# A transformer block's prelude: modulation weights by column halves, three pieces summed on TensorE, thirteen on VectorE

## The chip, the cores and the metric

The kernel runs on one core of a Trainium2 chip. The time is the device time of one execution in microseconds (us); lower is better. Times are medians over runs of the same kernel on the same inputs. The profile shows one execution, recorded by the hardware profiler. TensorE (PE) multiplies matrices, VectorE (DVE) and ScalarE (ACT) work element by element, GpSimd (POOL) does a few operations beside them, and SyncE (SP) issues the DMA transfers.

## The reference

The reference is one block of a hybrid model: sequence 1024, width 1024, batch 1, all in fp32. Cut to what matters here:

```python
mod = jax.nn.silu(c) @ w_mod[l] + b_mod[l]            # c is [1, 1024], w_mod [1024, 6144]
shift1, scale1, gate1, shift2, scale2, gate2 = jnp.split(mod, N_MOD, axis=-1)
u = modulate(rms_norm(h, ln1_g[l]), shift1, scale1)   # xn * (1 + scale) + shift
proj = u @ w_in                                        # then split: attention, RWKV, gates
...
h = h + gate1[:, None, :] * mix
u2 = modulate(rms_norm(h, ln2_g[l]), shift2, scale2)
h = h + gate2[:, None, :] * conv_ffn(u2, ...)
return rms_norm(h, final_g)
```

Nothing can be multiplied by `w_in` before `u` is there, and `u` needs `shift1` and `scale1`: 2048 columns of `w_mod`, 8 MB. This stretch, from the start to the first products with `w_in`, is the prelude.

## The kernel before, in words

**Form of the data.** `u` is held channel by row: `xn`, `u_hi` and `u_lo` are tiles of 128 partitions x 8 groups of channels (`kt`) x 1024 tokens. A number is split into a rounded part (`hi`, of type fp32r) and the rest (`lo`), and a product of two such numbers is three fp32r matmuls: hi by hi, lo by hi, hi by lo. A *block* `n` of the prelude is one `kt` and one half of the tokens (512); there are 16.

**The prelude's order.** It stands in one `with` block in which the order of SP, VectorE and ScalarE is the order of the program text (PE's is so in the whole kernel). Behind this block a scheduler orders VectorE, ScalarE, POOL and SP. The steps:

- `load_x` (L424) brings eight tiles of x, 128 tokens x 1024 channels, 512 KB each. `mod_load` (L428) brings sixteen pieces of `w_mod`, 128 rows x 1024 columns each: eight of the shift, then eight of the scale. `low_load` (L432) brings two weights of `w_in`, numbers 24 and 25. Buffers: three for pieces (`mw`), four shared by x tiles 0 to 3 and later pieces (`xa`), four for x tiles 4 to 7 and then one split weight (`xb`). A load into `xa` waits until the first four x tiles have been transposed.
- `square` (L438) and `norm_x` (L444) give each token its root mean square and scale x by it; `turn` (L450) transposes it on PE, four 128 x 128 transposes into a PSUM tile of two buffers, and ScalarE copies that to `xn`.
- `mod_add` (L455, L457) on VectorE multiplies a piece, row by row, by silu(c) and adds it to an accumulator, one for the shift and one for the scale. `mod_sum` sums an accumulator over its 128 partitions by one-column matmuls against ones; `mod_col` (L467, L469) adds the bias and forms `A1`, the factor of the modulation, and `m1`.
- `warm` issues matmuls whose result isn't used, into the PSUM tile `idle`.
- For each block: `u_full` scales and shifts `xn` on VectorE (L483) and casts it to `u_hi` on ScalarE (L484); `u_lower` takes the rest to `u_lo` on VectorE (L488); `low_part` multiplies the block by the three parts of weight 24 and of weight 25, into the PSUM tiles `low`. These are 96 matmuls, "the low matmuls" below. `low_split` (L499, L500) splits these two weights.
- Behind the blocks: `w2` is cast (`w2h`, ScalarE) and its rest taken on POOL (`w2l`), and `low_out` evicts the products.

**What follows.** The large matmuls with the other weights of `w_in` (`ps_rkv` in the profile) begin right behind the low matmuls on PE. Each weight comes through `load_w`: a load into `raw` (two buffers, also used by weights 24 and 25 and by `w2`), a cast on ScalarE (L268), the rest on VectorE (L270). Each use is 24 matmuls for 512 tokens.

Of the kernel before, what the change touches and what calls it, by code (L numbers as in the profile page):

```python
# [15 lines left out]
D = 1024  # L16
S = 1024
KT = 8
# [117 lines left out]
def hybrid_block(ctx: ExitStack, tc: tile.TileContext, a, out):  # L136
# [205 lines left out]
    with ExitStack() as es:  # L342
# [67 lines left out]
        with tc.tile_pool(name="st", bufs=1) as st, tc.tile_pool(name="stp", bufs=2, space=PS) as stp, \  # L410
# [3 lines left out]
            acc = [st.tile([128, D], F32, name=f"acc{seg}") for seg in range(2)]  # L414
            junk = acc[1]
            xn = st.tile([128, KT, S], F32, name="xn")
            xs, pieces = [], {}

            def ring(tag, name, dt=F32):
                return st.tile([128, D], dt, tag=tag, name=name, bufs=3 if tag == "mw" else 4)  # L420

            def load_x(t):
                xs.append(ring("xa" if t < 4 else "xb", f"xt{t}"))
                nc.sync.dma_start(xs[t], a["x"][t * 128 : t * 128 + 128, :])  # L424

            def mod_load(seg, ci):
                w = pieces[seg, ci] = ring("mw" if len(pieces) % 7 < 3 else "xa", f"wm{seg}{ci}")
                nc.sync.dma_start(w, a["w_mod"][ci * 128 : ci * 128 + 128, seg * D : seg * D + D])  # L428

            def low_load(i):  # L430
                raw = rp.tile([128, D], F32, tag="raw", name=f"raw_in{i}")
                nc.sync.dma_start(raw, a["w_in"][i])  # L432
                if i == 24:
                    return raw, *(wp.tile([128, D], F32R, tag=f"w{h}", name=f"{h}_in{i}", bufs=2) for h in ("hi", "lo"))
                return raw, *(ring("xb", f"{h}_in{i}", F32R) for h in ("hi", "lo"))

            def square(t):
                nc.scalar.activation(junk, xs[t], AF.Square, accum_out=ssq[:, t : t + 1])  # L438

            def norm_x(half):  # L440
                hs = slice(half * 4, half * 4 + 4)
                rms_rstd(rstd[:, hs], ssq[:, hs])
# [3 lines left out]
            def turn(kt, half):  # L446
# [3 lines left out]
                nc.scalar.copy(xn[:, kt, half * NH : half * NH + NH], ps)  # L450

            def mod_add(seg, ci, cols=slice(0, D)):
                w, s_ = pieces[seg, ci][:, cols], sc[:, ci : ci + 1]
                if ci == 0:
                    ts(acc[seg][:, cols], w, s_, None, op0=ALU.mult)  # L455
                else:
                    stt(acc[seg][:, cols], w, s_, acc[seg][:, cols], op0=ALU.mult, op1=ALU.add)  # L457

            def mod_sum(seg, k0, n):
                ps = pb.tile([128, NH], F32, tag="big", name=f"mod{seg}{k0}")  # L460
                for k in range(k0, k0 + n):
                    mm(ps[:, k : k + 1], acc[seg][:, k * 128 : k * 128 + 128], ones[:, 0:1], start=True, stop=True)
                return ps

            def mod_col(seg, k0, n, ps):
                k1 = slice(seg * 8 + k0, seg * 8 + k0 + n)
                tt(m1[:, k1], ps[:, k0 : k0 + n], V("b_mod", seg * 8 + k0, n), op=ALU.add)  # L467
                if seg:
                    stt(A1[:, k0 : k0 + n], m1[:, k1], 1.0, V("ln1_g", k0, n), op0=ALU.add, op1=ALU.mult)  # L469

            def warm(n, w=None):
                for _ in range(n):
                    if w is None:
                        mm(idle[:, 0:NC1], cst[:, 0:128], cst, start=True, stop=True)
                    else:
                        mm(idle, ones, w[:, 0:NH], start=True, stop=True)
# [4 lines left out]
            def u_full(n):  # L481
                kt, _, cs = block(n)
                ts(xn[:, kt, cs], xn[:, kt, cs], A1[:, kt : kt + 1], m1[:, kt : kt + 1], op0=ALU.mult, op1=ALU.add)  # L483
                nc.scalar.copy(u_hi[:, kt, cs], xn[:, kt, cs])  # L484

            def u_lower(n):
                kt, _, cs = block(n)
                tt(u_lo[:, kt, cs], xn[:, kt, cs], f32(u_hi[:, kt, cs]), op=ALU.subtract)  # L488

            def low_part(j, n):  # L490
                kt, half, cs = block(n)
                _, wh, wl = low[j]
                for i, (w, x) in enumerate(((wh, u_hi), (wl, u_hi), (wh, u_lo))):
# [3 lines left out]
            def low_split(j):  # L497
                raw, hi, lo = low[j]
                nc.scalar.copy(hi, raw)  # L499
                tt(lo, raw, f32(hi), op=ALU.subtract)  # L500
# [14 lines left out]
            order = [(seg, ci) for seg in range(2) for ci in range(KT)]  # L515
            for t in range(4):
                load_x(t)
            for m in range(3):
                mod_load(*order[m])
            for t in range(4, 8):  # L520
                load_x(t)
            warm(16)
            low = []

            def add_ahead(m):
                if m + 7 < 16:
                    if m + 7 == 14:
                        low.append(low_load(24))
                    mod_load(*order[m + 7])
                mod_add(*order[m])  # L530

            for t in range(4):
                square(t)
            norm_x(0)
            for m in range(3):
                mod_add(*order[m])
            for kt in range(KT):
                turn(kt, 0)
            for m in range(3, 10):
                mod_load(*order[m])  # L540
            for t in range(4, 8):
                square(t)
            for m in (3, 4):
                add_ahead(m)
            norm_x(1)
            for kt in range(KT):
                turn(kt, 1)
            nc.scalar.preload_act_table_set("sigmoid_and_others")
            for m in range(5, 15):
                add_ahead(m)  # L550
                if m == 7:
                    shift_ps = mod_sum(0, 0, KT)
                if m == 9:
                    mod_col(0, 0, KT, shift_ps)
                if m > 10:
                    warm(1, pieces[order[m]])
            low.append(low_load(25))
            low_ps = [[stp.tile([128, NH], F32, tag="low", name=f"low{j}{hf}", bufs=4) for hf in range(2)] for j in range(2)]
            low_split(0)
            halves_ = (slice(0, NH), slice(NH, D))  # L560
            for x in range(2):
                mod_add(1, KT - 1, halves_[x])
            scale_ps = [mod_sum(1, x * 4, 4) for x in range(2)]
            mod_col(1, 0, 4, scale_ps[0])
            u_full(0)
            mod_col(1, 4, 4, scale_ps[1])
# [6 lines left out]
            for n in range(16):  # L573
                if n < 15:
                    u_full(n + 1)
                u_lower(n)
                low_part(0, n)
                if n == 2:
                    low_split(1)
                if n == 3:  # L580
                    for m in range(3):
                        low_part(1, m)
                if n > 2:
                    low_part(1, n)
# [1421 lines left out]
```

## Time and profile before

| | us |
|---|---|
| median of 3 runs | 1670.34 |
| lowest and highest | 1670.2, 1674.31 |
| profiled execution, as timed | 1675.3 |
| its span, first to last instruction | 1673.2 |
| PE busy in the span | 1622.3 (97%) |
| DVE, ACT, POOL busy | 1227.8, 808.3, 147.8 |

How to read what is shown further down. In a *timeline* row stand start, length, engine, line, operation, result <- operands, shape, count of merged instructions, and in brackets how long the engine had been idle and what ended that. In the *chain of work* stand start, length, engine, tile: followed back from the last instruction, at each step to what released it. A row of *stretches* has the stretch, its length, then the busy time of PE, PEld (weight load), DVE, ACT and POOL with counts (or of one engine alone), the TensorE clock granted (1.00 is full), the share of the DMA engines and GB/s. A row of *groups* has line, engine, operation, tiles, shapes, count, then busy time in us and the mean of one in ns, then the idle time before them. Matmuls are pipelined, so a group's mean length is longer than the distance from one to the next. An fp32 matmul shows as two instructions, an fp32r matmul as one. A *DMA* row has packets, MB and the share that they took of 16 engines' time.

### The profile page before, as it was taken

What the parts mean: (1) busy time and instruction counts of PE and PEld (TensorE: products, weight loads), DVE (VectorE), ACT (ScalarE), POOL (GpSimd) and SP (SyncE); (2) the same over time, 40 slices, a digit from 0 to 9 for tenths busy, and PEclk for the clock granted to TensorE, in tenths of its full rate; (3) what the DMA queues carried; (4) which work ended last, traced back from release to release, by engine and by line L of the source; (5) the groups of instructions that cost most, each with busy time, mean ns of one, the idle gap of its engine ahead of it and who ended that gap; (6) DMA issues with size and microseconds to landing.
All of it is one profiled execution on the core that took longest, in us unless ns stands there. A gap on an engine that the chain in (4) does not pass through costs nothing.

```text
span 1673.2 us, 26056 instructions
## 1 busy us (share of the span) xinstructions
PE 1622.3 (97%) x9772; PEld 1333.2 (80%) x9772; DVE 1227.8 (73%) x2390; ACT 808.3 (48%) x1482; POOL 147.8 (9%) x175
## 2 busy tenths in 40 slices
PE   5899999999999998999999999999999999999998
PEld 4677877787977777888878888888888888888886
DVE  5786787888876635888778445897777777786677
ACT  5453343434455545767623244654444444455455
POOL 0010101111111012322022000000000000000000
PEclk8899999999999999999999999999999999999999
DMA  8497744433343236433197420143223323574463
GB/s 333 133 327 213 194 124 130 129 102 113 96 127 92 80 112 155 127 113 119 36 344 264 164 89 39 63 131 108 102 95 99 116 95 108 190 274 154 129 210 107
DMA packets 120974, 239.85 MB, mean 143 GB/s; under 512 B 39888, under 2 KB 48336, under 8 KB 120848
## 3 DMA queue, kind: packets, MB, share of 16 engines
q1 hardware_dynamic: 112896, 220.94, 40.8%
q0 software_dynamic: 7952, 17.25, 3.9%
q8 instruction: 77, 1.26, 0.3%
q14 instruction: 49, 0.40, 0.1%
HBM read 172.59 MB, written 65.54 MB: 142 GB/s over the span
## 4 chain that ended last, share of the span: by engine, by line
PE 82%; DVE 9%; DMA 4%; ACT 3%; issue 2%; SPq 1%; POOL 0%; DVEq 0%; ACTq 0%
PE X L144 13%; PE D L144 13%; PE Y L144 6%; PE gt L144 6%; PE ps_rkv L144 6%; PE wo L144 5%; PE br L144 5%; PE rk_ps L144 4%; PE W L144 3%; PE v L144 2%; PE lg L144 2%; PE ov L144 2%; PE tp L151 2%; PE qk L144 2%; PE low L144 1%
## 5 line engine op out<-in xcount | busy, mean ns | idle before, releaser
L144 PE MATMUL D<-op,op 128*128 128x512 f32 x924 | 209.8, 389 | 0.0
L144 PEld LDWEIGHTS D<-op,op 128*128 128x128 f32 x924 | 173.3, 188 | 36.3 <-DVE op L1269 0.3
L144 PE MATMUL X<-T_m,S 128*128 128x512 f32 x440 | 107.2, 390 | 0.1
L144 PEld LDWEIGHTS X<-T_m,S 128*128 128x128 f32 x440 | 82.4, 188 | 18.2 <-ACT T_m L1694 0.5
L1268 ACT CAST op<-g 128x512 fp32r<-128x512 f32 x77 | 47.8, 621 | 73.8 <-PE D L144 47.9
L1269 DVE TENSOR_TENSOR op<-g,op 128x512 fp32r<-128x512 f32 x77 | 53.0, 688 | 41.5 <-ACT op L1268 41.5
L1505 DVE SCALAR_TENSOR_TENSOR c<-ab,vec,c 128x512 f32<-128x512 f32 x88 | 65.8, 749 | 19.5 <-ACT c L1508 17.9
L1469 DVE TENSOR_TENSOR S<-ur,S 128x512 fp32r<-128x512 f32 x66 | 45.5, 691 | 35.9 <-ACT S L1465 35.7
L270 DVE TENSOR_TENSOR lo_in<-raw_in,hi_in 128x512 fp32r<-128x512 f32 x84 | 57.9, 727 | 14.0 <-PE gt L144 5.0
L1465 ACT CAST S<-ur 128x512 fp32r<-128x512 f32 x66 | 41.0, 622 | 55.8 <-DVE ur L1458 30.9
L1469 DVE TENSOR_TENSOR A<-ur,A 128x512 fp32r<-128x512 f32 x64 | 44.0, 687 | 30.9 <-ACT A L1465 30.7
L268 ACT CAST hi_in<-raw_in 128x1024 fp32r<-128x1024 f32 x42 | 43.9, 1048 | 44.4 <-PE ps_rkv L144 26.6
L740 DVE TENSOR_TENSOR t<-E,M 128x60 f32<-128x60 f32 (+24 forms) x248 | 56.0, 226 | 12.0 <-DMA M<-sm 5.7
L144 PE MATMUL Y<-T_h,A 128*128 128x512 f32 x264 | 63.5, 389 | 0.0
L144 PE MATMUL Y<-T_h,S 128*128 128x512 f32 x264 | 63.3, 389 | 0.0
L744 DVE TENSOR_TENSOR E<-E,t 128x60 f32<-128x60 f32 (+24 forms) x248 | 56.8, 229 | 5.8
L144 PE MATMUL X<-B_b,A 128*128 128x512 f32 x252 | 60.8, 390 | 0.0
L144 PE MATMUL W<-B_f,A 128*128 128x512 f32 x252 | 60.6, 389 | 0.0
L1090 ACT ACTIVATE P<-lg,nm 128x896 f32<-128x896 f32 (+3 forms) x64 | 47.4, 743 | 22.8 <-DVE nm L1086 22.6
L144 PEld LDWEIGHTS Y<-T_h,A 128*128 128x128 f32 x264 | 49.5, 188 | 10.4
L144 PEld LDWEIGHTS Y<-T_h,S 128*128 128x128 f32 x264 | 49.5, 188 | 10.3
L1465 ACT CAST A<-ur 128x512 fp32r<-128x512 f32 x64 | 39.8, 623 | 34.1 <-PE X L144 29.4
(473 smaller groups left out, 4151.9 us busy)
## 6 DMA issues: line engine op xcount, KB each, us to landing
raw_in<-in_w_in SPq DMA_DIRECT2D x50, 512.0 KB, 4.3
wm<-in_w_mod SPq DMA_DIRECT2D x48, 512.0 KB, 7.4
ur<-in_w_up SPq DMA_DIRECT2D x44, 512.0 KB, 4.3
g<-d_g SPq DMA_DIRECT2D x35, 512.0 KB, 3.9
d_g<-gs SPq DMA_DIRECT2D x44, 256.0 KB, 2.0
d_g<-c SPq DMA_DIRECT2D x33, 256.0 KB, 4.6
d_st<-qh SPq DMA_DIRECT2D x64, 128.0 KB, 2.4
d_gate<-gs SPq DMA_DIRECT2D x32, 256.0 KB, 2.7
```

The source lines that it names most:

```text
L144: weave.last = nc.tensor.matmul(o, lhsT, rhs, start=start, stop=stop, skip_group_check=more)
L151: nc.tensor.transpose(o, i, eye)
L268: nc.scalar.copy(hi, raw)
L270: nc.vector.tensor_tensor(lo[:, c : c + NH], raw[:, c : c + NH], f32(hi[:, c : c + NH]), op=ALU.subtract)
L740: i = tt(tv, E32[:, 0:J, s : s + 1].to_broadcast([128, J, W]), M32[:, s : s + 1, s + 1 : 32].to_broadcast([128, J, W]), op=ALU.mult)
L744: tt(E32[:, 0:J, s + 1 : 32], E32[:, 0:J, s + 1 : 32], tv, op=ALU.add)
L1090: nc.scalar.activation(e[:, 0:n], lg[:, 0:n], AF.Exp, bias=nm[:, 0:1], accum_out=nm[:, 1:2])
L1268: nc.scalar.copy(hi, src)
L1269: tt(lo, src, f32(hi), op=ALU.subtract)
L1465: nc.scalar.copy(hi, src)
L1469: tt(lo, src, f32(hi), op=ALU.subtract)
L1505: stt(c, ab[:, x + hf * NH : x + hf * NH + NH], V("conv_w", 22 * x + i), c, op0=ALU.mult, op1=ALU.add)
```

## The change

It concerns the prelude and one line of `load_w`.

- **Pieces.** A piece `m` is still 128 rows x 1024 columns, now 512 columns of the shift and the same 512 of the scale (two runs of 2 KB a row in place of one of 4 KB). Pieces 0 to 7 hold the first four channel groups (`side` 0), 8 to 15 the other four. There are four buffers `mw` for pieces 0 to 3 and 8 to 11, and the four of `xa` for 4 to 7 and 12 to 15. In the order of loads, x 4 to 7 stand behind piece 1, weight 24 ahead of piece 2, weight 25 behind piece 7.
- **Sums.** Pieces 0 to 2 are summed by PE: `scb` holds silu(c)/128 in all columns, `pe_add` multiplies a piece by it into two PSUM tiles, and ScalarE copies them to `bc`. Pieces 3 to 7 are summed on VectorE (`dve_add`), and `cols` adds both over the partitions into one PSUM tile. Pieces 8 to 15 are summed on VectorE, then by `cols`.
- **Order.** Of the first eight `turn`s VectorE copies six out of PSUM. When the first four channel groups have their `A1` and `m1`, blocks 0 to 7 are scaled and cast and multiplied by the hi and lo weights, while VectorE sums pieces 8 to 15; `u_lower` and the third product of these blocks come later, beside blocks 8 to 15.
- **Engines.** `u_full` runs on ScalarE for 14 of 16 blocks (scale, shift and cast), in place of VectorE and ScalarE.
- **Idle matmuls.** 12 in place of 16 at the start, 4 ahead of the blocks and 2 behind each of blocks 0 to 6, in place of one for each of four late pieces.
- **Next weights.** The cast of each later weight in `load_w` may stand in ScalarE's order only behind the matmuls of block 12. This is an order, not a wait.

The diff, cut to its core (unchanged helpers left out):

```diff
@@ load_w
-            nc.scalar.copy(hi, raw)
+            i = nc.scalar.copy(hi, raw)
+            if marks.get("pre"):
+                tc.add_manual_dep(i.ins, marks["pre"].ins.name, NOSYNC)
@@ the prelude's helpers
+            def mod_load():
+                m = len(pieces)
+                side, ci = m // 8, m % 8
+                pieces.append(st.tile([128, D], F32, tag="xa" if m // 4 % 2 else "mw", name=f"wm{m}", bufs=4)
+                              .rearrange("p (i c) -> p i c", i=2))
+                nc.sync.dma_start(pieces[m], a["w_mod"][ci * 128 : ci * 128 + 128, 0 : 2 * D]
+                                  .rearrange("p (i c) -> p i c", i=2)[:, :, side * NH : side * NH + NH])
...
+            def pe_add(m, ps, first, last):
+                for i in range(2):
+                    mm(ps[i], scb[:, m % 8, :], pieces[m][:, i, :], start=m == first, stop=m == last)
+
+            def dve_add(m, acc, first):
+                s_, w, f = acc[:, :, :], pieces[m][:, :, :], sc[:, m % 8 : m % 8 + 1]
+                if m == first:
+                    ts(s_, w, f, None, op0=ALU.mult)
                 else:
+                    stt(s_, w, f, s_, op0=ALU.mult, op1=ALU.add)
...
+            def u_full(n, on_act):
+                kt, _, cs = block(n)
+                if on_act:
+                    nc.scalar.activation(xn[:, kt, cs], xn[:, kt, cs], AF.Identity, scale=A1[:, kt : kt + 1], bias=m1[:, kt : kt + 1])
+                else:
+                    ts(xn[:, kt, cs], xn[:, kt, cs], A1[:, kt : kt + 1], m1[:, kt : kt + 1], op0=ALU.mult, op1=ALU.add)
                 nc.scalar.copy(u_hi[:, kt, cs], xn[:, kt, cs])
@@ the order: start and first half of x
+            for k in range(KT):
+                ts(scb[:, k, :], ones, sc[:, k : k + 1], 1.0 / 128, op0=ALU.mult, op1=ALU.mult)
...
+            scale_x(0)
+            for m in range(2):
+                pe_add(m, sum_l, 0, 2)
             for kt in range(KT):
+                if kt % 2 == 0:
+                    square(4 + kt // 2)
+                turn(kt, 0, nc.scalar.copy if kt in (2, 5) else nc.vector.tensor_copy)
+            for _ in range(4):
+                mod_load()
+            pe_add(2, sum_l, 0, 2)
+            rms_rstd(rstd[:, 4:8], ssq[:, 4:8])
+            scale_x(1)
+            low_hi(raw24, ...)
+            for i in range(2):
+                nc.scalar.copy(bc[:, i, :], sum_l[i])
+            raw25 = low_load(25)
...
+            cols(mod_ps, bc, True)
+            for m in range(3, 8):
+                dve_add(m, acc, 3)
+                if m > 3:
+                    turn(2 * m - 8, 1, nc.scalar.copy)
+                    turn(2 * m - 7, 1, nc.scalar.copy)
+                else:
+                    for _ in range(4):
+                        mod_load()
+            low_lo(0, raw24)
+            for _ in range(4):
+                mod_load()
+            low_hi(raw25, ...)
             nc.scalar.preload_act_table_set("sigmoid_and_others")
+            cols(mod_ps, acc, False)
+            mod_cols1(0, mod_ps)
...
+            u_full(0, False)
+            low_lo(1, raw25)
+            u_full(1, True)
+            acc = st.tile([128, 2, NH], F32, tag="acc", name="acc1")
+            warm(4)
+            for n in range(8):
+                if n < 6:
+                    u_full(n + 2, True)
+                low_part(0, n, (0, 1))
+                for k in (0, 1) if n == 1 else (n,) if n else ():
+                    low_part(1, k, (0, 1))
+                if n < 7:
+                    warm(2)
+                dve_add(8 + n, acc, 8)
+            cols(idle, acc, False, True)
+            for n in range(2):
+                u_lower(n)
+            for n in range(2):
+                for j in range(2):
+                    low_part(j, n, (2,))
+            mod_cols1(1, idle)
+            u_full(8, False)
             w2 = rp.tile([128, S], F32, tag="raw", name="w2")
...
+            u_full(9, True)
+            u_lower(2)
+            u_lower(8)
+            for n in range(8, 16):
+                if n < 14:
+                    u_full(n + 2, True)
+                if n < 14:
+                    for j in range(2):
+                        low_part(j, n - 6, (2,))
+                for j in range(2):
+                    low_part(j, n, (0, 1))
+                if n < 13:
+                    u_lower(n - 5)
                 if n < 15:
+                    u_lower(n + 1)
+                for j in range(2):
+                    low_part(j, n, (2,))
+                if n == 12:
+                    marks["pre"] = weave.last
```

More of the change, by code (lines that the diff above doesn't have):

```diff
@@ L459, in mod_sum @@
[L459 to L469, printed above, removed]
+                copy(xn[:, kt, half * NH : half * NH + NH], ps)
@@ new lines, in pe_add, with cols @@
+            def pe_add(m, ps, first, last):
[5 more added lines that the diff above has]
+                    ts(s_, w, f, None, op0=ALU.mult)
+                else:
+                    stt(s_, w, f, s_, op0=ALU.mult, op1=ALU.add)
+            def cols(ps, acc, first, last=False):
+                for k in range(4):
+                    for i in range(2):
+                        mm(ps[:, 2 * k + i : 2 * k + i + 1], acc[:, i, k * 128 : k * 128 + 128], ones[:, 0:1],
+                           start=(first or last) and k == 0 and i == 0, stop=not first, more=True)
@@ L549, in hybrid_block @@
[L549 to L557, printed above, removed]
-            low_ps = [[stp.tile([128, NH], F32, tag="low", name=f"low{j}{hf}", bufs=4) for hf in range(2)] for j in range(2)]
-            low_split(0)
-            halves_ = (slice(0, NH), slice(NH, D))
```

110 lines of the change are left out of this document (37 added, 73 removed).

## The prediction

> **What bounds the kernel now.** I read the chain of work that ended last first, up to 110 us, to see what the prelude hangs on.
>
> ```profile
> 33.49 8.91 DMA wm<-in_w_mod
> ...
> 45.12 3.56 PE mod L144 x16
> ...
> 55.61 21.57 PE low L144 x85
> 77.18 10.92 PE ps_rkv L144 x48
> ```
>
> The path runs over the last modulation piece, the column sums (PE mod), then the low matmuls, and at 77.2 us the large matmuls of the next stage follow without a gap. Next the busy time of each engine by stretch: is anything but TensorE a bound behind 77.2 us?
>
> ```profile
> 77.18:200.00 122.82, 120.01 (x584) 94.41 (x584) 89.99 (x151) 57.82 (x90) 12.93 (x18) 1.00 0.81 250
> ```
>
> PE is busy 120.0 of 122.8 us there (the page has 97% for the whole). So what is gained before 77.2 us should reach the end, and the prediction is a sum for the time at which the low matmuls end. Third, the same view of PE alone, in stretches cut where the granted clock (the column behind the busy time) changes:
>
> ```profile
> 11.90:15.30 3.40, 2.05 (x11) 1.00 1.02 417
> 46.10:49.50 3.40, 3.40 (x15) 0.50 0.86 240
> 49.50:52.90 3.40, 3.09 (x7) 0.50 0.35 136
> 52.90:56.35 3.45, 1.64 (x7) 0.99 0.22 50
> 59.80:77.20 17.40, 17.40 (x76) 1.00 0.33 104
> ```
>
> At full clock a low matmul takes 17.40/76 = 0.229 us, at half about 0.43. The clock is 0.52 in the stretch behind 11.90 to 15.30 and 0.51 in the one behind 52.90 to 56.35: 2.05 and 1.64 us of work in 3.4 were too little to hold it. The stretch of 3.09 us brought it back at 52.90. The one of 3.40 us from 46.10, mostly one-column matmuls, did not. Last, the timeline of the prelude:
>
> ```profile
> 6.51 5.49 PE L144 MATMUL idle<-cst 128*128 128x384 f32 x16 [6.51 <-DMA cst<-in_cst]
> 9.54 1.06 ACT L438 ACTIVATE acc<-xt 128x1024 f32<-128x1024 f32 x1
> 11.29 2.74 DVE L444 TENSOR_SCALAR xt<-xt,rstd 128x1024 f32<-128x1024 f32 x4 [7.90 <-ACT rstd L295]
> 19.62 12.22 SPq L428 DMA_DIRECT2D wm<-in_w_mod  x11
> 23.71 2.60 DVE L457 SCALAR_TENSOR_TENSOR acc<-wm,sc,acc 128x1024 f32<-128x1024 f32 x2 [6.38 <-DMA wm<-in_w_mod]
> 29.02 5.79 PE L151 MATMUL tr<-cst,xt 128*128 128x128 f32 x29 [0.18 <-DVE xt L444]
> 34.65 1.84 PE L144 MATMUL mod<-cst,acc 128*128 128x1 f32 x16
> 35.45 1.28 ACT L548 ACT_TABLE_LOAD   x1
> 36.35 2.82 PE L144 MATMUL idle<-wm,cst 128*128 128x512 f32 x6
> 36.61 6.56 DVE L457 SCALAR_TENSOR_TENSOR acc<-wm,sc,acc 128x1024 f32<-128x1024 f32 x5
> 48.65 0.80 PE L144 MATMUL low<-u_hi,hi_in 128*128 128x512 f32 x1
> ```
>
> All 96 low matmuls wait until 48.65 us, when all sixteen pieces are summed. They need 96 x 0.229 = 22.0 us and take 28.5.
>
> **The change, part by part.** *Loads.* Two queue states give the price of a piece in rows of 4 KB and of 2 KB, and one gives the worst packet found.
>
> ```profile
> DMA packets 441, 1.60 MB, mean 400 GB/s; under 512 B 50, under 2 KB 50, under 8 KB 441
> q1 hardware_dynamic: 441, 1.60, 101.8%
> ...
> DMA packets 144, 0.26 MB, mean 66 GB/s; under 512 B 16, under 2 KB 16, under 8 KB 144
> q1 hardware_dynamic: 144, 0.26, 17.4%
> ...
> DMA packets 394, 0.82 MB, mean 205 GB/s; under 512 B 161, under 2 KB 161, under 8 KB 394
> q0 software_dynamic: 250, 0.43, 65.2%
> q1 hardware_dynamic: 144, 0.40, 53.2%
> ```
>
> Each is a stretch of 4 us on 16 engines. The first (prelude, 24 us) gives 148 ns a packet, 0.52 MB in 1.3 us. The second, a store with 2 KB rows alone, gives 77 ns: the same rate. The third, two queues at once, gives 192 ns for packets of 2.1 KB on average. The halved pieces have 256 rows of 2 KB, so 16 packets an engine: 1.3 us by the nearest row, 3.1 us by the other end. I take 1.3. The fourth x tile is there at 9.54, so the pieces m0 and m1 land at 10.8 and 12.1, x to 17.3, raw24 18.6, m2 19.9, m3 21.2. m4 to m7 wait for the first transposes, as the eleven issues from 19.62 did, and the first of these reached VectorE 4.1 us later, at 23.71. SP meets no later wait: m11 needs the sum of m3, m12 to m15 those of m4 to m7, w2 the split of raw24, all done by 32 us.
>
> *First half of x.* Twelve instead of sixteen idle matmuls end at 6.5 + 12 x 0.343 = 10.6. A piece summed by PE is two fp32 matmuls, four instructions of 2.82/6 = 0.47: 1.9 us. Two pieces from 10.8, the first 1.1 us at half speed: 15.1. The eight scb multiplies lie in VectorE's 7.90 us of idleness ahead of 11.29. VectorE takes six of the eight copies out of PSUM:
>
> ```profile
> L634 DVE COPY z<-zp x8: 669/691/692, 133.2 to 144.1; 128x512 f32<-128x512 f32 x8
> L484 ACT CAST u_hi<-xn 128x512 fp32r<-128x512 f32 x16 | 9.8, 620 | 17.1 <-DVE xn L483 17.1
> L1508 ACT ACTIVATE c<-ab,vec 128x512 f32<-128x512 f32 x22 | 17.8, 813 | 1.3 <-DVE ab L1529 1.3
> ```
>
> At 0.69 us a copy and two buffers the eight turns take 5.3 us: 20.4. ScalarE does the second squares meanwhile. m4 then lands at 20.4 + 4.1 = 24.5, m7 at 28.4, raw25 at 29.7, m15 at 40.1.
>
> *Second half of x and the first columns.* PE adds m2 (20.4 to 22.3), ScalarE copies the two sums out (23.5), 16 one-column instructions take 1.84 us (25.3), the 32 transposes 32 x 5.79/29 = 6.4 (31.7). VectorE has scaled x by 24.2 (21.4 + 2.74) and sums m3 to m7 at 6.56/5 = 1.31 each by 30.1: not late. Column sums 33.5, their addition and the first scaling about 0.9 more. On ScalarE the last copy, the cast of raw25 and the table load of 1.28 us end at 34.6; the first u_hi is there at 35.2. Low matmuls start at **35.25 instead of 48.65**. The wait that is new is VectorE's for these columns: it splits raw24 until 31.3 and then stands idle to 33.5, and raw25's split and all eight sums of the second half are queued behind it. That is why those sums, though their pieces land from 31 us on, begin only at 35.6.
>
> *First eight blocks.* ScalarE now does both scaling and cast: 0.81 + 0.62 less some overlap = 1.35 us a block, u_hi(7) at 44.7. VectorE splits raw25 (35.6), then sums m8 to m15: 0.75 + 7 x 1.31, 45.6. PE needs 4 x 0.229 + 2 idle matmuls of 0.2 = 1.32 a block at full clock; the idle matmuls cost nothing only while ScalarE's 1.35 covers them. From 32.4 to 35.8 PE has some 2.3 us of work, a third of it one-column: by the row of 2.05 us I take the clock to be half from 35.8 to 39.2. Then block 1 ends at 39.2 (and its idle matmuls at 39.6), blocks 2 to 7 need 5 x 1.32 + 0.9: 47.1. That is later than VectorE's 45.6, so PE is the bound here.
>
> *Second half.* Column sums 48.9; addition, scaling and cast 1.6, partly under four matmuls of lower parts: 50.5. 60 of 96 matmuls are left: 13.7 us. Mostly one-column work from 46.1 to 49.5 lets the clock fall once more: 2.4 us at half cost 1.2. VectorE has two lower parts a block (1.2 us) and ScalarE 1.35 beside PE's 1.8, so neither is late. The low matmuls end at **65.4 instead of 77.2**.
>
> *Behind it.* The raw buffer of the second large weight comes free after u_hi(15), w2h and w2l:
>
> ```profile
> 69.64 2.54 POOL L588 TENSOR_TENSOR w2l<-w,w2h 128x512 fp32r<-128x512 f32 x2 [67.67 <-ACT w2h L585]
> ...
> wm<-in_w_mod SPq DMA_DIRECT2D x32, 512.0 KB, 7.9
> raw_in<-in_w_in SPq DMA_DIRECT2D x12, 512.0 KB, 4.2
> ```
>
> u_hi(15) 60.0, w2h 61.0, w2l 63.6, landed 67.8 by raw_in's 4.2 us, cast 68.9. PE wants it after 24 matmuls of the first weight, at 65.4 + 5.5 = 70.9: 2 us to spare. The cast of the first weight, ordered behind block 12's matmuls, costs at most its 1.05 us on ScalarE, which has that room; behind it stand the split on VectorE and, through the raw buffer, the third weight's load on SP, wanted only 11 us after the stage ends. I take nothing. POOL gets no new work.
>
> Sum: 77.2 - 65.4 = 11.8 us. The profiled execution has a span of 1673.2 and 1675.3 us in all, so 1663.5; against the median shown, 1670.34 (the profiled one lies 5 above it, near the highest of the three), **1658.5 us**.
>
> **The rule that speaks otherwise.** The Trainium skill, "TensorE: Matmul & The Clock Gate", Part 1, says the clock falls back only after at least one idle window of about 3.4 us. The stretch from 11.90, 2.05 us of work in it, contradicts that here. By the rule neither of my two falls would come.
>
> **Rivals.**
> 1. *The clock holds.* Idle matmuls fill the gaps: blocks follow ScalarE to 45.6, columns 47.4, u_hi(8) 49.0, end 62.7: 14.5 us less, 1655.8. For it: the work of 32.4 to 35.8 lies between the rows of 2.05 and 3.09. Chance 0.17.
> 2. *Given back in part.* One more half-rate stretch at 11.9 (the first sums, 1.7 us), or the second weight landing in 7.9 us as wm does instead of 4.2, a PE stall of 1.7, and VectorE's backlog behind the stage grown by as much: 4 to 7 us lost, about 1664. Chance 0.20.
> 3. *It does not start early.* At 160 ns a 2 KB packet a piece takes 2.56 us. 9.5 + 16 x 2.56 + 6 x 1.3 = 58.3 for m15; 1.3 for its sum, 1.84 for columns, 1.6, 13.7: 76.7. No change, 1670. Chance 0.11.
> 4. *Slower: the 2 KB rows.* At the 192 ns of the third queue state a piece takes 3.07 us, m15 lands at 66.5, the low matmuls end at 84.9: 7.7 us more, 1678. It decides from about 182 ns on. Against it: that row has two queues with half the packets each, while the prelude's row at 24 us shows one queue and 400 GB/s. Chance 0.07.
>
> The forecast keeps 0.45.
>
> **How the numbers follow.** This kernel's runs tell 0.3%, 5 us, from no change. Faster by more: forecast and rivals 1 and 2, 0.82. Same: rival 3, 0.11. Slower: rival 4, 0.07. The range reaches from a held clock with 2 us more from the next stage, 1653.5, to rival 2 with all its losses and a little more, 1667; outside lie rivals 3 and 4 and a sliver.
>
> **What would show it.** Right: first low matmul near 35 us, a row of summing m8 to m15 ending near 45.6, low matmuls ending at 63 to 66, the large ones without a gap after them. Wrong: VectorE waiting on wm for m5 to m15 (packets over 100 ns); ScalarE over 1.5 us a block or a table load inside the blocks; granted clock 0.5 beyond 40 us and 53 us; a PE wait on the second weight or on VectorE between 66 and 80 us.

## The result, and the profile after

The first comparison gave 1664.07 us for the changed kernel (five runs, 1660.97 to 1665.54) beside 1670.82 for the one before (five runs, 1670.2 to 1674.43): a ratio of 0.995 [0.9933, 0.9967]. Two later batches repeated both: 1661.36 against 1674.26, 0.9926 [0.9911, 0.994], and 1663.62 against 1674.42, 0.993 [0.9916, 0.9943]. The changed kernel is faster by 7 to 13 us, 0.5 to 0.7%. The kernel before ran over 50 more times in the later batches, with medians of 1674.1 to 1674.4, so its first runs had been low; why is not shown.

| one profiled execution each | before | changed |
|---|---|---|
| first low matmul, us | 48.65 | 34.43 |
| low matmuls end | 77.02 | 62.54 |
| span | 1673.2 | 1658.9 |
| span less the end of the low matmuls | 1596.2 | 1596.4 |

The span is 14.3 us shorter and the low matmuls end 14.5 us earlier: in this pair the whole gain lies in the prelude, and what stands behind it is as long as before. The profiled execution of the kernel before (1675.3) is slower than all five of its first comparison, and that of the changed kernel (1660.97) is the fastest of its five, so 14.3 us is more than the medians give. The ends here are the starts of the first large matmul (`ps_rkv`).

The chain of work of the changed kernel, in the same columns as before:

```profile
9.71 10.77 DMA wm<-in_w_mod
20.52 2.00 PE suml L144 x4
...
32.47 1.28 ACT L573
33.76 0.62 ACT u_hi L489
...
45.23 1.69 PE idle L144 x16
46.95 0.19 DVE m L469
...
48.56 14.14 PE low L144 x60
62.70 10.91 PE ps_rkv L144 x48
```

The path still begins with a modulation piece, but with the third (m2) and not the last. PE sums it, a table load on ScalarE (L573) stands just ahead of the first `u_hi`, the blocks run to 45.23, the second columns (16 one-column matmuls, tile `idle`) follow, and 60 low matmuls run on end.

The timeline shows what ran beside the blocks:

```profile
34.43 0.50 PE L144 MATMUL low<-u_hi,hi_in 128*128 128x512 f32 x1 [1.06 <-ACT u_hi L489]
35.39 9.21 DVE L459 SCALAR_TENSOR_TENSOR acc<-wm,sc,acc 128x1024 f32<-128x1024 f32 x7
56.04 1.03 ACT L268 CAST hi_in<-raw_in 128x1024 fp32r<-128x1024 f32 x1
74.64 2.08 PE L144 MATMUL ps_rkv<-u_hi,hi_in 128*128 128x512 f32 x8 [1.05 <-DVE sh_rkv L361]
```

VectorE's seven sums take 9.21 us without a wait for a piece, wholly beside PE's blocks. The first large weight's cast (L268) runs at 56.04, amid blocks 8 to 15. And the stretches of PE, with the granted clock behind the busy time:

```profile
29.80:33.20 3.40, 3.40 (x28) 1.00 1.03 386
33.20:36.60 3.40, 2.05 (x8) 1.00 1.05 393
36.60:40.00 3.40, 3.40 (x17) 1.00 1.08 349
46.85:50.25 3.40, 2.79 (x12) 1.00 0.01 5
50.25:53.65 3.40, 3.40 (x16) 1.00 0.00 0
```

Neither of the two falls of the clock that the forecast took came in this execution, though one stretch held only 2.05 us of work. A fall that it did not take did come: the clock was at half from 26.4 to 29.8 us, under the transposes of the second half of x (in a second trace, after_again, from 25.4 to 28.8). Two variants further down, no_pre and hold, are the same program up to the blocks and kept the clock there; their first low matmul comes at 33.34 and 33.18 us, about 1 us earlier.

### The profile page after: what moved, and what is told of

Its sections match the earlier page's. It is cut to its first block, busy times and chain, and to the rows that moved or that the text cites. A ratio compares the mean times of both kernels' runs of the same rounds, so it can differ in the third digit from the quotient of the medians.

```text
span 1658.9 us, 26127 instructions
## 1 busy us (share of the span) xinstructions
PE 1620.1 (98%) x9806; PEld 1332.3 (80%) x9806; DVE 1223.2 (74%) x2385; ACT 816.1 (49%) x1492; POOL 149.2 (9%) x175
## 4 chain that ended last, share of the span: by engine, by line
PE 84%; DVE 8%; ACT 3%; DMA 3%; issue 1%; SPq 1%; DVEq 0%; ACTq 0%
PE X L144 13%; PE D L144 13%; PE Y L144 6%; PE gt L144 6%; PE ps_rkv L144 6%; PE wo L144 5%; PE br L144 5%; PE rk_ps L144 4%; PE W L144 3%; PE v L144 3%; PE qk L144 2%; PE lg L144 2%; PE ov L144 2%; PE tp L151 2%; PE low L144 1%
## 5 line engine op out<-in xcount | busy, mean ns | idle before, releaser
L272 DVE TENSOR_TENSOR lo_in<-raw_in,hi_in 128x512 fp32r<-128x512 f32 x84 | 58.0, 730 | 17.2 <-PE gt L144 7.8
L268 ACT CAST hi_in<-raw_in 128x1024 fp32r<-128x1024 f32 x42 | 44.0, 1049 | 46.0 <-PE ps_rkv L144 28.1
L1129 ACT ACTIVATE P<-lg,nm 128x896 f32<-128x896 f32 (+3 forms) x64 | 47.5, 744 | 22.2 <-DVE nm L1125 22.0
L144 PEld LDWEIGHTS Y<-T_h,A 128*128 128x128 f32 x264 | 49.5, 188 | 10.4
L144 PEld LDWEIGHTS Y<-T_h,S 128*128 128x128 f32 x264 | 49.6, 188 | 10.3
```

Of the source, the lines that this page charges most:

```text
L144: weave.last = nc.tensor.matmul(o, lhsT, rhs, start=start, stop=stop, skip_group_check=more)
L268: i = nc.scalar.copy(hi, raw)
L1129: nc.scalar.activation(e[:, 0:n], lg[:, 0:n], AF.Exp, bias=nm[:, 0:1], accum_out=nm[:, 1:2])
```

## The experiments

Two questions were left. Which parts carry the gain? And why did the three comparisons differ by 6 us: does the clock in the prelude make the runs differ (theory P), or does what follows the prelude move by itself (rival R)? All variants, with one trace each; "rest" is the span less the end of the low matmuls:

| kernel | first low | low end | span | rest | median us | ratio to before |
|---|---|---|---|---|---|---|
| before_again | 49.47 | 76.29 | 1669.6 | 1593.3 | 1671.65 (one run) | |
| after_again | 34.35 | 62.47 | 1659.5 | 1597.0 | 1661.36 | 0.9926 [0.9911, 0.994] |
| no_fill | 34.09 | 63.77 | 1662.3 | 1598.5 | 1664.31 | 0.994 [0.9922, 0.9958] |
| no_pre | 33.34 | 66.75 | 1663.4 | 1596.7 | 1666.53 | 0.9962 [0.995, 0.9975] |
| sums_dve | 38.15 | 66.82 | 1670.5 | 1603.7 | 1671.11 | 0.9987 [0.9978, 0.9995] |
| lower_early | 34.03 | 67.09 | 1662.5 | 1595.4 | 1664.89 | 0.9947 [0.9934, 0.9959] |
| pre8 | 34.28 | 65.92 | 1664.0 | 1598.1 | 1665.1 | 0.9943 [0.9929, 0.9957] |
| before_fill | 48.53 | 75.33 | 1669.4 | 1594.1 | 1673.22 | 1.0001 [0.999, 1.0012] |
| before_fill2 | 48.12 | 75.19 | 1672.0 | 1596.8 | 1674.88 | 1.0001 [0.9991, 1.0011] |
| hold | 33.18 | 63.05 | 1659.3 | 1596.3 | 1660.76 | 0.9914 [0.9901, 0.9928] |
| best_hold | 34.01 | 63.19 | 1653.6 | 1590.4 | 1661.94 | 0.9921 [0.9904, 0.9937] |
| after_third | 35.44 | 64.61 | 1659.0 | 1594.4 | 1663.62 | 0.993 [0.9916, 0.9943] |

The first four rows are one batch, then four, then four with after_third; within a batch the runs of the kernel before are shared.

### Both kernels once more

No edit.

> The kernel before once more, for a second trace. Theory P (the spread of a kernel's runs lies in the prelude, because the half-rate stretches of the TensorE clock fall at another phase in each execution): the low matmuls end 1 to 4 us from the 77.0 us of the first trace, and what lies behind them, 1596.2 us there, stays within 0.5 us. Rival R (the prelude is steady, the rest varies): the end stays within 0.5 us of 77.0, and the rest moves by 1 to 4 us.

> The changed kernel once more, for a second trace and more times. Theory P: the low matmuls end 1 to 3 us behind the 62.5 us of the first trace, with a half-rate stretch that the first trace lacks, and the rest stays within 0.5 us of 1596.4. Rival R: the end stays within 0.5 us of 62.5 and the rest is longer by 2 to 5 us, as the median lies 3 us above the profiled execution. Time 1664 by both.

> The changed kernel a third time, on the chip of the three kernels beside it. Two traces of it ended the low matmuls at 62.5 us with the clock held from 30 us on; a variant that is the same up to block 8 lost it at 33.3 us and ended at 65.9. Theory (the clock is on the edge there: the same program holds it in some executions and loses it in others): times spread over 1660 to 1666, and this trace ends at 62.5 or, where it lost the clock, at 64 to 66. Rival (the loss belongs to that variant): end 62.4 to 62.6 again and all times within 2 us.

The three traces of the changed kernel end the prelude at 62.54, 62.47 and 64.61. The third differs in two places. The first sums on PE (tile `suml`) take 5.94 us in place of 3.67 and 3.90, with single instructions of up to 1.19 us (0.67 and 0.90 in the others):

```profile
10.92 5.94 PE L144 MATMUL suml<-wm,xwa 128*128 128x512 f32 x8 [0.70 <-DMA wm<-in_w_mod]
```

The clock of this trace is first recorded at full at 15.5 us, that of the other two at 9.4 and 11.7, so these sums ran mostly at half clock (ahead of the first record the views show 1.00 all the same). That is the first item of the forecast's rival 2. At the first low matmul this trace is 1.0 us behind the first one (35.44 against 34.43), and not more, as it kept the clock under the transposes. The other place is what the forecast had taken for its first fall (stretches of PE):

```profile
32.35:35.75 3.40, 2.52 (x18) 1.00 1.05 397
35.75:39.30 3.55, 3.55 (x10) 0.53 1.05 387
```

The forecast put the half-rate clock from 35.8 to 39.2; here it is, and the columns start at 47.1 as forecast. So P is true as far as it goes: the clock, in these two places together, moves the end of the prelude by some 2 us. But the span is 1659.0, like that of the two others, because the rest is 2.0 to 2.6 us shorter. R is true as well: with nothing changed behind the prelude the rest was 1594.4, 1596.4 and 1597.0 in the changed kernel, 1593.3 and 1596.2 in the one before. In all five traces the stretch from the first W matmul to the first D matmul lasts 426.4 to 426.7 us and from there to the end 217.4; the differences lie ahead, in the scheduled stages. Neither theory holds in the form in which it was put down, with the one part steady within 0.5 us. One profile therefore settles a difference of 2 or 3 us in no direction.

### The order of the next weights' copies

```diff
-                if n == 12:
-                    marks["pre"] = weave.last
```

> The changed kernel without the order of the next weights' casts behind block 12. Forecast: the order costs and brings nothing; the cast and the split of the first large weight (1.05 us on ScalarE, 1.3 us on VectorE) move ahead among the blocks, PE has slack of 0.4 us a block there, the end stays within 0.5 us of 62.5 and the time within 1.5 us. Rival (the order carries part of the gain): the cast sits among the first eight blocks, where ScalarE's 1.37 us a block is the bound, u_hi(7) and all behind it come 1 to 2.3 us later, and the time is up by as much.

Without the order the kernel is 5.2 us slower than the changed one in the same batch (1666.53 against 1661.36; each of its 12 runs, from 1663.61 up, is slower than each of the changed kernel's six, up to 1662.81), and the prelude ends 4.3 us later. The second columns start at 45.08 us, as in the changed kernel (45.07), so this loss lies behind them. The timelines of ScalarE, VectorE and PE show why:

```profile
47.53 1.05 ACT L268 CAST hi_in<-raw_in 128x1024 fp32r<-128x1024 f32 x1 [4.63 <-DMA raw_in<-in_w_in]
48.60 1.29 DVE L272 TENSOR_TENSOR lo_in<-raw_in,hi_in 128x512 fp32r<-128x512 f32 x2 [3.69 <-ACT hi_in L268]
49.81 0.16 DVE L469 TENSOR_TENSOR m<-idle,vec 128x8 f32<-128x8 f32 x1
51.41 1.22 PE L144 MATMUL low<-u_lo,hi_in 128*128 128x512 f32 x2 [3.46 <-DVE u_lo L493]
```

In this kernel the cast of the first large weight stands on ScalarE ahead of block 8's `u_hi`, and it waits 4.63 us for a load that ends at 47.5. VectorE's split of that weight (L272) waits for the cast and stands ahead of `m`, the second columns; PE is idle for 3.46 us. The clock falls behind that gap (0.51 from 50.9 to 54.3) and costs more. Engines work in their order: a wait for something that is wanted late becomes a wait for all that is queued behind it. In the changed kernel the same cast, at 56.04, has its data and nobody waits. The forecast for this run was wrong, and the rival had the place wrong and the price too low: the cast stands behind the first eight blocks, not among them, and what costs is its wait for the load.

```diff
-                if n == 12:
+                if n == 8:
```

> The changed kernel with the next weights' casts ordered behind block 8 instead of 12. Theory (without the order it is the wait for a weight that has not landed, ahead of the second columns, that costs, not the cast's and the split's own 1.05 and 1.3 us): the weight landed at 47.5 us where the order was taken away, so behind block 8 nothing waits for it; end within 0.4 us of 62.5, time the changed kernel's. Rival (the cast and the split cost their own time among the blocks): end 63.5 to 65.

Ordered behind block 8 already, the cast runs at 52.37 and shows no wait, yet the trace ends the prelude at 65.92. The loss begins earlier, where the two programs are still the same; the second columns start at 46.90 in place of 45.07 (stretches of PE):

```profile
29.82:33.25 3.43, 3.40 (x27) 0.99 1.05 388
33.25:36.70 3.45, 2.42 (x6) 0.51 1.05 391
```

The 60 last matmuls take 1.6 us more as well (15.54 us from the first of them to the first large matmul, in place of 13.98): the clock falls once more, from 50.4 to 53.8, behind a stretch that ends ahead of the cast. Of six runs the fastest, 1660.93, is near the changed kernel's fastest (1659.66 to 1660.97 in its three batches). The median, 1665.1, lies 1.0 to 3.7 us above the changed kernel's three and 1.4 under that without the order. Whether block 8 or 12 matters was not settled; what this trace lacks is the wait.

### The idle matmuls

```diff
-            warm(4)
...
-                if n < 7:
-                    warm(2)
```

> The changed kernel without the 4 and the 7 x 2 idle matmuls of the first eight blocks; the output is the same. Theory C (they hold the clock, as the forecast's rival 1 has it): without them PE has 0.92 us of work in each 1.37 us, the clock falls to half inside the blocks, a block takes 1.7 us, and the low matmuls end 2 to 4 us later than 62.5; time 1666 to 1668. Rival (the low matmuls hold it alone, or the clock is no matter here): end 62.0 to 62.6, time as the changed kernel's.

The stretches of PE without them:

```profile
31.50:34.90 3.40, 1.49 (x9) 1.00 1.05 398
34.90:38.30 3.40, 2.83 (x7) 0.51 1.05 387
45.20:48.60 3.40, 2.79 (x19) 1.00 0.20 80
48.60:52.00 3.40, 3.40 (x10) 0.51 0.00 0
```

Both falls of the forecast come here, behind 1.49 and behind 2.79 us of work (the second at 48.6, forecast 49.5). The first costs little, since ScalarE with 1.37 us a block sets the pace then: the second columns start at 44.72, no later than in the changed kernel. The second lies among the 60 last matmuls and costs 1.6 (15.56 us to the first large matmul in place of 13.98). The prelude ends 1.3 us later, less than the theory's 2 to 4. The time is 1664.31 against 1661.36 in the same batch; the rest of this trace is 1.5 us longer too.

The opposite, more idle matmuls ahead of the blocks and in the gap behind the second columns:

```diff
-            warm(4)
+            warm(8)
...
+            for _ in range(4):
+                mm(mod_ps[:, 128:NH], cst[:, 0:128], cst, start=True, stop=True)
             mod_cols1(1, idle)
```

> The changed kernel with 8 instead of 4 idle matmuls ahead of the first block and 4 more ahead of block 8, in gaps that PE has anyway (1.1 and 0.6 us). Theory of the edge: the clock is held in more executions; end 62.4 to 62.7, median 1 to 2 us below the changed kernel's in the same call and no time over 1664. Rival (what is lost is not the clock, or 8 at half rate take 2.7 us and delay the first block): median the same or above.

The median is 1660.76, five runs from 1658.68 to 1661.41, beside 1663.62 (1660.72 to 1664.53) for the changed kernel in the same batch. Its median is the lowest seen. Against the changed kernel's 1661.36 of another batch it gains only 0.6, and the two ratios' intervals overlap, so an advantage is likely but not certain. The stretches of its trace show that the second fall was not kept away:

```profile
43.70:47.10 3.40, 3.27 (x23) 1.00 0.51 190
47.10:50.50 3.40, 3.40 (x10) 0.50 0.01 2
```

3.27 us of work, 16 instructions of it one-column matmuls, lost the clock; without these it was 1.44 us.

> The same with three small moves: the table load ahead of the transposes' copies of the second half, piece 8 summed on VectorE while it waits for the first columns (into the space of scb), block 1 scaled on VectorE. Theory (ScalarE at 1.37 us a block, VectorE's eight sums and PE are bounds of the first eight blocks within 0.5 us of each other, so relieving two of them brings little): first low matmul at 34.0 to 34.2, the column sums start at 44.0 to 44.6 instead of 45.07, end 61.6 to 62.0; time 0.5 to 1 us below the kernel with more idle matmuls, which the times hardly tell. Rival (one of them is the bound alone): end 60.5 to 61.3.

This adds three moves to the version above. The table load stands right behind the `bc` copies, piece 8 is scaled ahead of the columns, and block 1 is scaled on VectorE:

```diff
+            nc.scalar.preload_act_table_set("sigmoid_and_others")
...
-            nc.scalar.preload_act_table_set("sigmoid_and_others")
             cols(mod_ps, acc, False)
+            acc = xwa.rearrange("p (i c) -> p i c", i=2)
+            dve_add(8, acc, 8)
             mod_cols1(0, mod_ps)
...
+            u_full(1, False)
             low_lo(1, raw25)
-            u_full(1, True)
-            acc = st.tile([128, 2, NH], F32, tag="acc", name="acc1")
```

VectorE's timeline shows the last two rows of the sums:

```profile
34.81 7.88 DVE L459 SCALAR_TENSOR_TENSOR xwa<-wm,sc,xwa 128x1024 f32<-128x1024 f32 x6
42.87 1.28 DVE L459 SCALAR_TENSOR_TENSOR xwa<-wm,sc,xwa 128x1024 f32<-128x1024 f32 x1 [0.18 <-DMA wm<-in_w_mod]
```

The second columns start at 44.21, as was expected, but the trace of the version above has them at 44.11 without these moves: in both the last sum waits for the last piece, which lands at 42.7. From there the clock fell at 46.85, 60 matmuls took 14.65 us, and the prelude ends at 63.19 in place of the expected 61.6 to 62.0. Its profiled execution, 1653.6 us of span, is the shortest of all, but by a rest of 1590.4, and the median, 1661.94 (1655.64 to 1664.64), is no gain over the version before.

### Three pieces on TensorE

```diff
-                pe_add(m, sum_l, 0, 2)
+                dve_add(m, acc, 0)
...
-            pe_add(2, sum_l, 0, 2)
+            dve_add(2, acc, 0)          # behind scale_x(1)
-            cols(mod_ps, bc, True)
-            cols(mod_ps, acc, False)
+            cols(mod_ps, acc, False, True)
```

(`scb`, `bc` and the copies go with them.)

> The changed kernel with pieces 0 to 2 summed on VectorE as well, none on PE. Theory (PE's three sums shorten the way to the first columns): VectorE gets 3.3 us more, its sum of piece 7 ends at 32.4 instead of 29.7, the first low matmul comes at 36 to 36.5 instead of 34.4, the low matmuls end at 64 to 66; time 1.5 to 3.5 us above the changed kernel's. Rival (the stage hangs on loads and transposes, the sums are beside it): first low matmul within 0.4 us of 34.4, end 62.3 to 63, time the same.

VectorE's timeline and the stretches of PE:

```profile
25.47 7.88 DVE L459 SCALAR_TENSOR_TENSOR acc<-wm,sc,acc 128x1024 f32<-128x1024 f32 x6
36.49 0.17 DVE L469 TENSOR_TENSOR m<-mod,vec 128x8 f32<-128x8 f32 x1 [2.00 <-PE mod L144]
34.10:37.50 3.40, 3.40 (x16) 0.50 1.07 394
```

With all eight pieces on VectorE its sums end at 33.3, the columns run at half clock, and the first scaling factor is there at 36.5 in place of 32.6. The low matmuls begin 3.7 us later and end 4.3 us later. So the sums on PE are worth up to 4 us of the prelude, the clock's share in them. The median loses more, 1671.11, only 3 us under the kernel before. The trace has a rest of 1603.7, 7 us more than the changed kernel's, and they are spread: 3.2 from the prelude's end to the first matmul of the tile `gt`, 2.3 from there to `rk_ps`, 1.8 from there to `W`. Some of VectorE's work behind the prelude stands in another order in this variant; the loads are issued in the same order. Whether that is the cause of the 7 us was not settled.

### The lower parts late

```diff
-                low_part(0, n, (0, 1))
+                u_lower(n)
+                low_part(0, n)
```

(likewise for weight 25; the later `u_lower` and third products of blocks 0 to 7 go.)

> The changed kernel with the lower parts of blocks 0 to 7 and their third product made in the first loop, not left late. Theory (VectorE is a bound of the first loop, so what is put on it there comes out whole): 8 lower parts of 0.6 us make the sum of piece 15 end near 49 to 50 instead of 44.6, 12 of the 60 matmuls behind it are gone, the low matmuls end at 64 to 64.5; time 1.5 to 2 us above the changed kernel's. Rival (PE's work is the same, so is the end): end within 0.5 us of 62.5.

The timelines of VectorE and PE:

```profile
46.86 1.28 DVE L459 SCALAR_TENSOR_TENSOR acc<-wm,sc,acc 128x1024 f32<-128x1024 f32 x1
51.56 0.17 DVE L469 TENSOR_TENSOR m<-idle,vec 128x8 f32<-128x8 f32 x1 [3.43 <-PE idle L144]
49.69 1.84 PE L144 MATMUL idle<-cst,acc 128*128 128x1 f32 x16
```

The sum of the last piece ends at 48.1 in place of 44.6, as eight lower parts stand between the sums. But then VectorE waits 3.43 us for PE: with three products a block, and with the clock at half from 35.1 to 38.5, PE ends its blocks only at 49.69, and the columns run behind them. So in this execution PE was the bound of the first loop, not VectorE as the theory has it. `m` follows at 51.6 in place of 46.95. Fewer matmuls are left then, and the low matmuls end at 67.09. The trace ran at half clock again from 52.1 to 58.9, so the share of the order alone can't be read from it. The median, 1664.89, is 1 to 4 us above the changed kernel's three; how much of that is the order and how much the clock stays open.

### The clock alone, on the kernel before

Idle matmuls put into the kernel before, in the first version 12 ahead of the column sums, 8 ahead of block 3 and 2 behind each of blocks 0 to 2; in the second 14 in place of 12, and 10 more ahead of them:

```diff
+                if m == 13:
+                    warm(10)
...
+            warm(14)
...
+                if n == 3:
+                    warm(8)
...
+                if n < 3:
+                    warm(2)
```

> The kernel before with idle matmuls in PE's gaps: 12 ahead of the scale's column sums, 2 behind each of blocks 0 to 2, 8 ahead of block 3. Theory (a part of the gain is the clock alone): the columns take 1.84 us instead of 3.56, no half-rate stretch falls between 43 and 60 us, the low matmuls end at 72 to 73.5 instead of 76.3 to 77.0, and the time is 3 to 5 us below the kernel before. Rival (before, the blocks hang on VectorE, so the clock is no matter): end 75.5 to 77.

> The kernel before with idle matmuls from 39 us on, so that those ahead of the columns run at full clock (12 of them at half rate took 4 us and came late in the first try): 10 ahead of piece 13's, 14 ahead of the scale's columns, then 2 behind each of blocks 0 to 2 and 8 ahead of block 3. Theory (part of the gain is the clock alone): columns at full clock, first low matmul at 47.0 instead of 48.65, no half-rate stretch between 40 and 77 us, end 72 to 73.5, time 3 to 5 us below the kernel before. Rival (VectorE's 1.06 us a block and the split of weight 25 bound these blocks before): end 74.5 to 76.5, time within 2 us of the kernel before.

Both measure 1.0001, no difference, and the ends of 72 to 73.5 us that the theories name did not come. In the first the 12 idle matmuls themselves ran late and at half clock. In the second the clock held from 32.7 to 49.6 us (rows of its stretches):

```profile
39.50:42.90 3.40, 3.14 (x12) 1.00 0.63 253
42.90:46.30 3.40, 3.01 (x21) 1.00 0.09 19
46.30:49.60 3.30, 2.27 (x14) 1.00 0.82 239
49.60:52.90 3.30, 3.30 (x10) 0.50 0.40 155
```

The end of its low matmuls comes 1 to 2 us earlier than in the traces of the kernel before, and that is lost in the rest. The first low matmul still starts at 48.12: full clock does not bring the last piece sooner. So the clock up to 49.6 us is not what the change gains by; a prelude of the kernel before with full clock to its end was not measured, as the clock fell again from 49.6 to 53.

What the change gains is the earlier start. In its own trace the sum of the last piece ends at 44.6 us and 32 of the 96 low matmuls have run by 45.1; before, none ran until all sixteen pieces were summed. That is read from the waits. No run had pieces of whole width with the rest of the change, and none had `u_full` back on VectorE for all blocks, so what these two parts are worth alone is open.

## Why the prediction was right

The range (1653.5 to 1667) holds all three medians, and the 11.8 us of the forecast stand beside 6.8, 12.9 and 10.8 measured. Point by point:

- **What bounds the kernel.** Right. 14.5 us gained ahead of the large matmuls gave 14.3 of span. Where variants move the prelude by 2 us, though, the rest's own spread, 3.7 us in five traces of the two kernels, hides it.
- **Loads.** Right. A stretch of the changed kernel in which the pieces land, 22 to 35 us, shows:

```profile
DMA packets 2460, 5.01 MB, mean 385 GB/s; under 512 B 149, under 2 KB 149, under 8 KB 2459
q1 hardware_dynamic: 2459, 4.99, 102.7%
```

  1.027 x 16 x 13 / 2459 is 87 ns a packet, 1.39 us a piece, against 1.3 taken, 2.56 in rival 3 and 3.07 in rival 4. The two rivals of 2 KB rows fall. The last piece, forecast for 40.1, lands at 42.7 where a trace shows it (hold); VectorE gets to it at 43.3 in the changed kernel, so this cost nothing, but only 0.6 us of earlier sums was left to win there.
- **First half.** m2 is summed by 22.5 (22.3), the new wait of VectorE for the columns ends at 32.6 (33.5), the first low matmul runs at 34.43, 34.35 and 35.44 (35.25). ScalarE's chain with the table load sets it, as forecast, in the first two traces. In the third, where the first sums ran late, it is VectorE's sums and the columns: the table load ends at 34.6, and `u_hi` waits until 34.77 for the scaling.
- **First eight blocks.** ScalarE takes 1.37 us a block (1.35), VectorE's sums end at 44.6 (45.6), columns start at 45.2 where the clock held and at 47.1 where it fell once (47.1).
- **The two falls.** This is the mis-sized term. The forecast took both; the three traces had none, none and the first. The ends are 62.5, 62.5 and 64.6 instead of 65.4: rival 1's prelude (62.7) in two of three. Two of three ends lie below the 63 to 66 that the forecast names as a sign of being right. Both falls are real possibilities, since variants with nearly the same PE work show them; but which comes was luck, and so is the nearness of 11.8 to the measured 10.8 and 12.9.
- **Second half.** 60 matmuls take 14.14 us (13.7, and 1.2 for the fall). The large matmuls follow with no gap. PE waits 1.05 us for VectorE ahead of 74.6, which the forecast lists among the signs of being wrong; it is for evictions of the large products, and the kernel before has 0.96 us of it ahead of 89.05, just as far behind its low matmuls.
- **The order of the next weights' copies.** "I take nothing" was right as its cost, as far as the traces show: PE has no gap between the low and the large matmuls. What the forecast did not see is what it protects: without it 5.2 us of the gain go.
- **The median.** The sum from the profiled execution's own time gave 1663.5, and the first comparison has 1664.07. Moving it to 1658.5 rested on a median of three runs, 1670.34, some 4 us below that of all later runs. From 1674.3 the same 11.8 would give 1662.5, amid 1661.4 to 1664.1. By the same base rival 1's 14.5 us would give 1659.8, lower than any median of this kernel. So two errors partly cancelled in 1658.5: a base about 4 us too low, and a gain 2.7 us too small where the clock held.

On the clock, the Trainium skill, "TensorE: Matmul & The Clock Gate", Part 1, has it fall only after an idle window of about 3.4 us. Where the clock held through 2.05 us of work the trace agrees. It disagrees where the clock fell behind 3.27 us (hold), 2.52 (after_third) and 3.40 us of work (pre8): none of these windows was idle. But the forecast's own reading, that too little work loses the clock, explains no better why 2.05 held it in one trace and 3.40, mostly small matmuls, lost it in another, as long as all of PE's busy time is counted; the last section counts it another way.

## What to carry to other kernels

When a product waits for a sum over all of a load, order the load by the part of the output that it completes: half of the columns let half of the work start, and the rest of the load runs beside it. When work for a later stage may be queued among critical work, look at what each of its first instructions waits for; one cast that waits for a late load holds up every instruction behind it on its engine, and through it on the others. And take more than one trace of each kernel before a term of 2 us is believed: two equal programs differed by that much here, in the prelude and behind it.

## What the runs showed of the hardware

The granted clock went two ways for the same instructions. The changed kernel and the variant pre8 are the same program up to block 8; the stretches from 29.80 and from 29.82 both have 3.40 us of busy PE, with 28 and 27 instructions; then the one ran on at 1.00 and the other at 0.51. 2.79 us of work lost the clock in no_fill and kept it in the changed kernel. So the busy time of a stretch does not tell which comes. The stretches that lost it in spite of more than 3 us of work held many one-column matmuls; but the one from 29.80, which kept it, held them too.

Leaving the one-column matmuls out sorts the traces much better. Up to 65 us the recorded half-rate stretches last 3.41 us or two or three times that. The full-clock time of all 14 traces, from the first recorded change of each to 65 us and cut in the same steps, makes 164 stretches, and 34 of them end with a fall:

| PE's work in a stretch of 3.41 us, one-column matmuls left out | lost the clock | kept it |
|---|---|---|
| up to 1.50 us | 22 | 0 |
| 1.51 to 2.08 us | 12 | 17 |
| 2.09 us and more | 0 | 113 |

With all busy time counted, the clock was lost behind 0.39 to 3.34 us and kept behind 1.74 to 3.41, so that most values go both ways. The pairs above fall into place: the 2.79 us of no_fill are about 1.6 without the one-column matmuls, those of the changed kernel stay 2.79; the stretch from 29.8 has 1.87 us in the changed kernel and 1.78 in pre8, in the band where both happen; the 2.05 us of the changed kernel hold no one-column matmul at all. This sorts traces that were there; no run changed the one-column matmuls alone.
